# An encoder layer on one core: w_out's parts kept for three passes, a hand-written order of the engines up to the first up tile, and modulation pieces in other places

## The chip, the core and the metric

The kernel runs on one core of a Trainium2 chip. The metric is the device time of one execution in microseconds (us); the median of three executions before the change is 1642.57 us (1640.33 to 1643.46). Four compute engines matter: TensorE (PE) multiplies matrices, VectorE (DVE) and GpSimd (POOL) do elementwise work, ScalarE (ACT) applies functions and copies. SyncE (SP) issues the transfers, in order, on one queue.

## What is computed

One layer with a token mixer and a channel mixer, on 1024 tokens of 1024 features; six modulation rows (shift, scale and gate for each half) come from a small product of a condition vector with w_ada.

```
mod = (silu(c) @ w_ada + b_ada);  sh1, sc1, g1, sh2, sc2, g2 = split(mod, 6)
h = rmsnorm(x) * (1 + sc1) + sh1
z = h @ w_in                                   # q, k, v of three attentions, gates
ya, yb, yc = attention A (chunks), B (forgetting), C (top-k)
merged = sum over b of sigmoid(gate_b) * (y_b @ w_branch[b])
x = x + g1 * rmsnorm(merged @ w_out)
h = rmsnorm(x) * (1 + sc2) + sh2
a, g = split(h @ w_up)                         # 2 x 2816 features
x = x + g2 * rmsnorm((gelu(conv3(a)) * g) @ w_down)
```

## The kernel before

Every large product is made of float32 numbers split in a high and a low part; three matmuls (high x high, high x low, low x high) give one product. Activations stand feature-major (128 features in the partitions, 1024 tokens along), in 8 feature tiles; tokens come in 8 blocks of 128.

Time runs through these stages. Attention (A, B, C with four heads each) runs with a background list, `items`: the projections, 20 early gates (`early_gate`) and modulation pieces (`ada_item`, lines 567 to 576) are worked off a step at a time between the heads' instructions, at a rate per head (`tick`). A modulation piece reads two 128-column strips of w_ada (1 MB, two loads), takes eight VectorE operations over them (`ada_steps`), one GpSimd sum, two small matmuls and two VectorE operations (`ada_end`). There are 16 such pieces for the rows 2 to 5: eight are in `items` (`N_ADA`), the other eight in the merge (lines 1010 to 1016), three per branch.

The merge (lines 972 to 1016) goes over 3 branches x 8 feature tiles: w_branch's parts are split, 12 matmuls per tile make the product, VectorE multiplies it with the gate (line 1000), GpSimd adds it into M (line 1002), and in the last branch M is split and written to DRAM (`M_spill`). Four gates of the last branch (`late_gate`) are made here, 48 matmuls each.

Then w_out (`proj_tokens`, line 1032) in three passes over blocks (0, 1, 2), (3, 4, 5) and (6, 7). A pass loads all eight 128-row strips of w_out again, splits each (ScalarE the high part; GpSimd and VectorE in turn the low part), reads M's strip back (`merged`, in the five places of tag `e`), and makes 6 matmuls per block and strip. `normed` normalises a block's sum from PSUM and adds it to x; `second_norm` normalises again, transposes a block in 8 small matmuls (`xT2`, in the three PSUM banks of tag `n`), applies the modulation and makes the left operands of a seven-product scheme (A11, A12, S1, S2, S4, S3, A22), two blocks (even and odd) for one index i of each left operand. These operands lie in `big` (the two places that held the layer's normalised input) and three `left_S` tiles. The passes' late parts are interleaved in the program with the next pass.

The up projection (`up_tile`, line 1215) goes over 22 feature tiles of a and g: seven products of 12 matmuls each, from `up_weights` (two loads, then right operands B11, B21, T1, T2, B22, T3, T4). The first tile is made in two halves, columns 0 to 255 (blocks 0 to 3) and 256 to 511 (blocks 4 to 7), so that it can start before the last blocks are done. The convolution, GELU and the product follow, and the result goes to DRAM in left operands of the down projection, which is five chunks of seven products (`PLAN`, line 1402), and final blocks. The row of g2 is spread over the partitions (`mod_row(5, ...)`, line 1476) after the first product.

The order of instructions on the engines is made by a planner, from the program's order and modelled times, outside of `manual_schedule`; inside such a section the order of the named engines is the program's own. The planner also allots places (buffers of a tag) and the order of SP's queue in both.

```
    ada_todo = [(a, a + 1) for v in (2, 3, 4, 5) for a in range(v * 8, v * 8 + 8, 2)]
...
    for n_p, blocks in enumerate(((0, 1, 2), (3, 4, 5), (6, 7))):
        o3 = proj_tokens(KD, merged, w_out, blocks, "ddsssn", f"wo{n_p}", 2, (pool, dve))
```

Of the kernel before, what the change touches and what calls it, by code (L numbers as in the profile page):

```python
# [33 lines left out]
N_ADA = 8  # L34
ADA_FROM = 1
# [26 lines left out]
def encoder_layer(ctx: ExitStack, tc: tile.TileContext, x, w_ada, w_in, w_branch, w_out, w_up, w_down,  # L62
# [140 lines left out]
    def ada_end(srcs, acc, tag="n", eng=pool):  # L203

        eng.tensor_tensor(acc[:, 0], acc[:, 0], acc[:, 1], op=OP.add)
        pm = bank(tag, "ada_ps")
# [7 lines left out]
    def ada_piece(srcs, per_k, tag="n"):  # L214
        for acc in ada_steps(per_k):
            pass
        ada_end(srcs, acc, tag)
# [347 lines left out]
    ada_todo = [(a, a + 1) for v in (2, 3, 4, 5) for a in range(v * 8, v * 8 + 8, 2)]  # L565
# [404 lines left out]
    ada_next = None  # L970
    M = [None] * KD
    for b in range(3):
# [5 lines left out]
        for m in range(KD):  # L978
# [31 lines left out]
            if b or m:  # L1010
                if ada_next is not None:
                    ada_piece(*ada_next)
                ada_next = None
# [18 lines left out]
    def proj_tokens(n_k, operand, w, blocks, banks, name, stagger, engs):  # L1032


        tags = iter(banks)
        o = [[bank(next(tags), f"{name}o{t}{e}") for e in range(2)] for t in range(len(blocks))]
        ts_ = slice(blocks[0] * P, (blocks[-1] + 1) * P)
        ops = []
        for k in range(n_k):
            raw = raw4(f"{name}raw{k}", (P, D))  # L1040
            nc.sync.dma_start(raw, w[k * P:(k + 1) * P, :])
            wh, wl = split(raw, (P, D), f"{name}w{k}", engs[k % len(engs)])
            s = operand(k, ts_)
            ops.append((s, wh, wl))
            if k < n_k - stagger:
                steps = [(k, t) for t in range(len(blocks))]
            elif k < n_k - 1:
                continue
            else:
                steps = [(kk, t) for t in range(len(blocks)) for kk in range(n_k - stagger, n_k)]  # L1050
            for kk, t in steps:
                s_, wh_, wl_ = ops[kk]
                tk = slice(t * P, (t + 1) * P)
                for e in range(2):
                    es = slice(e * HALF, (e + 1) * HALF)
                    pe.matmul(o[t][e], s_[:, 0, tk], wh_[:, es], start=(kk == 0), stop=False)
                    pe.matmul(o[t][e], s_[:, 0, tk], wl_[:, es], start=False, stop=False)
                    pe.matmul(o[t][e], s_[:, 1, tk], wh_[:, es], start=False, stop=(kk == n_k - 1))
        return o

    def normed(o, g_row, x1, tmp, name):
# [9 lines left out]
        r = rstd_of(ss, name)  # L1071
        dve.scalar_tensor_tensor(x1, tmp, r, x1, op0=OP.mult, op1=OP.add)
# [19 lines left out]
    h_even = [None]  # L1092

    def second_norm(x1, xn2, tb):
        ss = sm(f"s2_{tb}")
        act.activation(xn2, x1, AF.Square, accum_out=ss)
        r = rstd_of(ss, f"n2_{tb}")
        dve.tensor_scalar(xn2, x1, r, None, op0=OP.mult)
        h32 = (k4 if tb % 2 else f4)(f"h2_{tb}", F32, (P, KD, P))
        for g in range(2):  # L1100
            pt = bank("n", f"xT2_{tb}_{g}")
            for kk in range(4):
                k = g * 4 + kk
# [78 lines left out]
    for n_p, blocks in enumerate(((0, 1, 2), (3, 4, 5), (6, 7))):  # L1182
# [4 lines left out]
        if UP_POS == n_p == 2:  # L1187
            r_first = up_weights(0)
# [339 lines left out]
```

## Time and profile before

| what | value |
|---|---|
| median of 3 executions | 1642.57 us (1640.33 to 1643.46) |
| the profiled execution's own time | 1643.54 us |
| its span, first to last instruction | 1641.7 us |
| TensorE busy | 1513.8 us (92%) |
| VectorE / ScalarE / GpSimd busy | 1207.4 / 805.7 / 594.4 us |
| moved by DMA | 262.37 MB, mean 160 GB/s |
| mean granted clock of TensorE | 0.973 |

The page's picture of the span in 40 equal slices (tenths busy, clock in tenths, 9 for 90% or more):

```
PE   3989999989999999987999849999999999999997
DVE  6766898998678526589536894878777877877768
PEclk9999999999999999998999969999999999999999
```

One slice is 41 us. Read the picture for where TensorE's row falls below 9: at the start, once in attention, in slices 18 and 19 (700 to 780 us, the merge) and 23 and 24 (940 to 990 us, from w_out to the first up tile).

### The profile page before, as it was taken

Reading aid. Unit: us, or ns where it says so; the run is one execution under the profiler, and the core shown is the slowest. Engines: PE = TensorE matmul, PEld = TensorE weight load, DVE = VectorE, ACT = ScalarE, POOL = GpSimd, SP = SyncE. Lnnn points to the kernel's source line nnn. Section 1 sums busy time; section 2 is a strip of 40 time slices with the busy share of each in tenths; the row PEclk is TensorE's granted clock in tenths of the full one; section 3 lists DMA queues with packets and bytes.
Section 4 is the critical chain, followed back from the end, with each engine's and each line's share of the span. In section 5 each row is a group of like instructions: output and inputs, shape, how many; then the busy total and the mean of one; then the engine's idle time right before and its main releaser. Section 6 shows DMA issues by size and latency. Waiting matters only on the chain. (4 is left out here: it accounts for less than half of the span.)

```text
span 1641.7 us, 21382 instructions
## 1 busy us (share of the span) xinstructions
PE 1513.8 (92%) x7322; PEld 1247.1 (76%) x7322; DVE 1207.4 (74%) x2174; ACT 805.7 (49%) x1482; POOL 594.4 (36%) x420
## 2 busy tenths in 40 slices
PE   3989999989999999987999849999999999999997
PEld 2768888777887888765777737778888888788885
DVE  6766898998678526589536894878777877877768
ACT  4434698776544546521235653555555555532212
POOL 3432534443544434116344641222222322432205
PEclk9999999999999999998999969999999999999999
DMA  9442332435452222295668711445444444987752
GB/s 284 123 103 52 97 104 81 155 104 163 122 153 67 77 94 89 86 320 174 211 252 280 241 64 52 141 141 175 146 154 142 141 141 150 407 304 256 260 187 103
DMA packets 190175, 262.37 MB, mean 160 GB/s; under 512 B 15147, under 2 KB 145395, under 8 KB 190067
## 3 DMA queue, kind: packets, MB, share of 16 engines
q1 hardware_dynamic: 190067, 261.01, 48.0%
q8 instruction: 58, 0.95, 0.2%
q14 instruction: 50, 0.41, 0.1%
HBM read 178.14 MB, written 74.97 MB: 154 GB/s over the span
## 5 line engine op out<-in xcount | busy, mean ns | idle before, releaser
L199 DVE SCALAR_TENSOR_TENSOR ada_acc<-ada_raw,c_act,ada_acc 128x256 f32<-128x256 f32 x144 | 99.0, 732 | 4.9 <-DMA ada_raw<-in_w_ada 4.8
L647 ACT ACTIVATE junk<-sc,thr 128x512 bf16<-128x512 f32 (+2 forms) x93 | 80.2, 862 | 30.8 <-DVE thr L668 25.8
L1170 POOL TENSOR_TENSOR T<-ua,ug 128x512 f32<-128x512 f32 x22 | 29.2, 1327 | 175.2 <-DVE rT L1156 166.1
L649 DVE TENSOR_SCALAR_CACHE_REDUCE junk<-sc,thr 128x384 bf16<-128x384 f32 (+2 forms) x93 | 89.6, 964 | 1.8
L1251 POOL TENSOR_TENSOR cv<-cv,g 128x1024 f32<-128x1024 f32 x22 | 58.0, 2639 | 59.2 <-ACT cv L1250 42.5
L1211 PE MATMUL X<-left_S,rT 128*128 128x512 f32 (+1 forms) x184 | 70.8, 385 | 0.5 <-ACT p L1228 0.5
L1213 PE MATMUL X<-left_S,rT 128*128 128x512 f32 (+1 forms) x184 | 70.6, 384 | 0.0
L1212 PE MATMUL X<-left_S,rT 128*128 128x512 f32 (+1 forms) x184 | 70.6, 384 | 0.0
L1471 DVE TENSOR_TENSOR acc<-acc,X 128x512 f32<-128x512 f32 x68 | 46.0, 685 | 24.2 <-PE X L1468 24.2
L1166 POOL TENSOR_TENSOR ug<-ug 128x512 f32<-128x512 f32 x22 | 30.0, 1363 | 86.7 <-DVE ua L1162 86.7
L1341 ACT ACTIVATE T<-work 128x512 fp32r<-128x512 f32 x40 | 25.0, 630 | 59.7 <-PE X L1468 19.6
L1471 DVE TENSOR_TENSOR acc<-acc,V 128x512 f32<-128x512 f32 x56 | 38.1, 685 | 18.0 <-PE V L1468 17.3
L1155 ACT ACTIVATE rT<-ug 128x512 fp32r<-128x512 f32 x44 | 27.5, 625 | 48.3 <-PE X L1213 24.9
L1211 PE MATMUL X<-big,rB 128*128 128x512 f32 (+1 forms) x92 | 36.3, 395 | 15.0 <-DVE xn L1068 14.2
L1467 PE MATMUL X<-T,ring 128*128 128x512 f32 x120 | 47.1, 393 | 0.0
L1466 PE MATMUL X<-T,ring 128*128 128x512 f32 x120 | 46.8, 392 | 0.0
L1468 PE MATMUL X<-T,ring 128*128 128x512 f32 x120 | 46.5, 389 | 0.0
L1156 DVE TENSOR_TENSOR rB<-ua,rB 128x512 fp32r<-128x512 f32 x44 | 37.7, 862 | 9.2 <-ACT rB L1155 8.3
L530 ACT ACTIVATE tg<-g,gate_b 128x512 f32<-128x512 f32 x48 | 32.5, 679 | 22.7 <-PE g L249 22.5
L1156 DVE TENSOR_TENSOR rT<-ug,rT 128x512 fp32r<-128x512 f32 x44 | 33.4, 760 | 12.6 <-ACT rT L1155 12.6
L1341 ACT ACTIVATE B<-wd 128x512 fp32r<-128x512 f32 x26 | 16.4, 631 | 51.8 <-DVE acc L1471 25.9
L1155 ACT ACTIVATE rB<-ua 128x512 fp32r<-128x512 f32 x44 | 27.3, 627 | 29.3 <-PE V L1213 22.3
(1096 smaller groups left out, 5660.0 us busy)
## 6 DMA issues: line engine op xcount, KB each, us to landing
ring<-L_spill SPq DMA_DIRECT2D x70, 512.0 KB, 5.4
L_spill<-S SPq DMA_DIRECT2D x40, 512.0 KB, 4.3
ada_raw<-in_w_ada SPq DMA_DIRECT2D x32, 512.0 KB, 4.5
L_spill<-A SPq DMA_DIRECT2D x30, 512.0 KB, 3.3
raw_g<-in_w_in SPq DMA_DIRECT2D x24, 512.0 KB, 4.1
ua<-in_w_up SPq DMA_DIRECT2D x22, 512.0 KB, 4.0
ug<-in_w_up SPq DMA_DIRECT2D x22, 512.0 KB, 3.8
gate_spill<-tg SPq DMA_DIRECT2D x20, 512.0 KB, 2.6
```

Of the source, the lines that this page charges most:

```text
L199: dve.scalar_tensor_tensor(acc[:, k % 2], per_k[k], c_act[:, k:k + 1], acc[:, k % 2], op0=OP.mult, op1=OP.add)
L647: act.activation(junk_a[:, 0:n], scores[b], AF.Sign, scale=-1.0, bias=t_f, accum_out=cnt[:, j:j + 1])
L649: dve.tensor_scalar(junk_d[:, 0:n], scores[b], t_f, None, op0=OP.is_lt, op1=OP.add, accum_out=cnt[:, j:j + 1])
L1155: act.activation(hl_[0], src, AF.Copy)
L1156: eng.tensor_tensor(hl_[1], src, hl_[0].bitcast(F32), op=OP.subtract)
L1211: pe.matmul(oc, r[:, 0, k], lh, start=(first and k == 0), stop=False, skip_group_check=True)
L1212: pe.matmul(oc, r[:, 0, k], ll, start=False, stop=False, skip_group_check=True)
L1213: pe.matmul(oc, r[:, 1, k], lh, start=False, stop=(last and k == 3), skip_group_check=True)
L1251: pool.tensor_tensor(cv, cv, g, op=OP.mult)
L1466: pe.matmul(o, lh, r[:, 0], start=(starts and k == 0), stop=False, skip_group_check=True)
L1467: pe.matmul(o, lh, r[:, 1], start=False, stop=False, skip_group_check=True)
L1471: dve.tensor_tensor(dst, dst, o, op=OP.add)
```

## The change

w_out's strips are loaded and split once, in pass 0. Strip 0's parts lie in two places of tag `w4`; the parts of strips 1 to 7 lie in places of the left operands for i = 2 and 3, which blocks 4 to 7 fill later. Pass 2 goes over the strips in the order 1, 2, 5, 6, 0, 3, 4, 7. From pass 1 to the last product of the first up tile the order on ScalarE, VectorE, GpSimd and TensorE is written out by hand; SP's is still planned. Even blocks' left operands are made by one ScalarE copy and one VectorE subtraction of double width. The first up tile's right operands lie in other places, `up_weights` gives its steps one by one, and `up_tile` stops after each product. Twelve modulation pieces are in `items` and none in the merge; the four pieces of row 5 are loaded and made in the first three chunks of the down projection, and its row is spread in the fourth.

```
-N_ADA = 8
-ADA_FROM = 1
+ADA_AT = (1, 2, 3, 4, 5, 6, 7, 8, 11, 13, 15, 17)
...
-    ada_todo = [(a, a + 1) for v in (2, 3, 4, 5) for a in range(v * 8, v * 8 + 8, 2)]
+    ada_todo = [(a, a + 1) for v in (2, 3, 4) for a in range(v * 8, v * 8 + 8, 2)]
...
         items.append(early_gate(i))
-        if i >= ADA_FROM and len(ada_todo) > 16 - N_ADA:
+        if i in ADA_AT:
             items.append(ada_item(ada_todo.pop(0)))
...
-            if b or m:
-                if ada_next is not None:
-                    ada_piece(*ada_next)
-                ada_next = None
-                if ada_todo and m in (1, 3, 5):
-                    a = ada_todo.pop(0)
-                    ada_next = (a, ada_load(a, lambda n, shape: f4(n, F32, shape)))
...
+    def wo_load(k, eng):
+        raw = raw4(f"wo_raw{k}", (P, D))
+        nc.sync.dma_start(raw, w_out[k * P:(k + 1) * P, :])
+        if k == 0:
+            hi, lo = (w4(f"wo0{j}", (P, 2, HALF)) for j in "hl")
+        else:
+            hi, lo = (left[n][:, :, i].rearrange("p e k c -> p e (k c)") for n, i in PLACES[2 * k - 2:2 * k])
+        src = raw.rearrange("p (e c) -> p e c", e=2)
+        act.activation(hi, src, AF.Copy)
+        eng.tensor_tensor(lo, src, hi.bitcast(F32), op=OP.subtract)
+        wo.append((hi, lo))
+
+    PLACES = [(n, i) for ns in (("A11", "A12", "A22", "S1"), ("S2", "S4", "S3")) for i in (2, 3) for n in ns]
+
+    class Pass:
+        def __init__(self, n_p, blocks, order):
+            self.n_p, self.blocks, self.order = n_p, blocks, order
+            tags = iter("ddsssn")
+            self.o = [[bank(next(tags), f"wo{n_p}o{t}{e}") for e in range(2)] for t in range(len(blocks))]
+            self.m = {}
+
+        def step(self, n, ts=None):
+            k = self.order[n]
+            if k not in self.m:
+                self.m[k] = merged(k, slice(self.blocks[0] * P, (self.blocks[-1] + 1) * P))
...
+                    pe.matmul(self.o[t][e], s_[:, 0, tk], hi[:, e], start=(n == 0), stop=False)
+                    pe.matmul(self.o[t][e], s_[:, 0, tk], lo[:, e], start=False, stop=False)
+                    pe.matmul(self.o[t][e], s_[:, 1, tk], hi[:, e], start=False, stop=(n == KD - 1))
...
+        def lefts_even(self):
+            h = self.h.rearrange("p (a k) c -> p a k c", a=2)
+            t = big[0]
+            act.activation(t[:, :, 0, self.i], h, AF.Copy)
+            dve.tensor_tensor(t[:, :, 1, self.i], h, t[:, :, 0, self.i].bitcast(F32), op=OP.subtract)
...
-    R0 = dict(B11=e4, B21=e4, T1=e4, T2=w4_first, B22=w4_first, T3=k4_first, T4=raw4)
+    R0 = dict(B11=e4, B21=e4, T1=e4, T2=w4_first, B22=w4_first, T3=w4_first, T4=w4_first)
...
+    pass0 = Pass(0, (0, 1, 2), range(KD))
+    for k in range(KD):
+        wo_load(k, (pool, dve)[k % 2])
+        if k < KD - 2:
+            pass0.step(k)
+    for t in range(3):
+        for k in (KD - 2, KD - 1):
+            pass0.step(k, (t,))
...
+    with tc.manual_schedule(engines={E.Activation, E.DVE, E.Pool, E.PE}):
+        b0, b1, b2 = blocks(0, 1, 2)
+        pass1 = Pass(1, (3, 4, 5), range(KD))
+        b0.normed(pass0.o[0])
+        b0.residual()
+        b1.normed(pass0.o[1])
+        b0.norm2()
+        b1.residual()
+        b0.scaled()
+        b2.normed(pass0.o[2])
+        b1.norm2()
+        pass1.step(0)
+        b0.turn()
+        b1.scaled()
+        b2.residual()
+        b0.modulated()
...
+        r, ws = up_weights(0)
+        go(ws)
+        for n in (4, 5, 6):
+            pass1.step(n)
+        go(ws, 3)
+        b3, b4, b5 = blocks(3, 4, 5)
+        for t in range(3):
+            pass1.step(7, (t,))
+
+        pass2 = Pass(2, (6, 7), (1, 2, 5, 6, 0, 3, 4, 7))
+        b3.normed(pass1.o[0])
+        b3.residual()
+        b4.normed(pass1.o[1])
+        b3.norm2()
+        b4.residual()
+        b3.scaled()
+        b5.normed(pass1.o[2])
+        b4.norm2()
+        pass2.step(0)
+        b4.scaled()
+        b5.residual()
+        b5.norm2()
+        pass2.step(1)
+        b3.turn()
+        b3.modulated()
+        left3 = b3.lefts_odd(b2)
+        go(left3)
+        b5.scaled()
+        pass2.step(2)
+        b4.turn()
+        b4.modulated()
+        go(left3)
+        pass2.step(3)
+        b5.turn()
...
+        pass2.step(6)
+        pass2.step(7, (0,))
+        b6, b7 = blocks(6, 7)
+        b6.normed(pass2.o[0])
+        pass2.step(7, (1,))
+        b6.residual()
+        b7.normed(pass2.o[1])
+        b6.norm2()
+        first = up_tile(0, r, PARTS0)
+        go(first)
+        b7.residual()
+        b6.scaled()
+        go(first)
+        b7.norm2()
+        go(first, 3)
+        b6.turn()
+        b6.modulated()
+        b7.scaled()
+        go(first)
+        b6.lefts_even()
+        b7.turn()
+        b7.modulated()
+        go(first)
...
+    G2_AT = {0: (40,), 1: (42, 44), 2: (46,)}
...
+            if n == 0:
+                for a in G2_AT.get(c, ()):
...
+            if n == 5:
+                for a in G2_AT.get(c, ()):
+                    ada_piece((a, a + 1), ada_in[a], pm=VB[a // 2 % 2])
+                if c == 3:
+                    mod_row(5, G2, VB)
```

`Block` holds the steps that `normed` and `second_norm` made before: `normed` (squares, products with g1's row, the root), `residual` (adds x, writes x1), `norm2` (square and root), `scaled`, `turn` (8 transposes), `modulated`, `lefts_odd` and `lefts_even`; `go` draws the next step of a generator.

## Rows read from the trace of the kernel before

**Rows 1.** Busy time by stretch: stretch, length, five engines (instructions), TensorE's clock, DMA.
```profile
702.00:732.00 30.00, 28.88 (x120) 22.40 (x121) 26.16 (x58) 6.42 (x14) 2.26 (x3) 0.94 0.99 334
732.00:776.00 44.00, 32.43 (x116) 23.34 (x114) 43.71 (x59) 6.66 (x12) 24.73 (x12) 0.88 0.57 183
776.00:841.50 65.50, 63.48 (x275) 52.20 (x276) 30.88 (x39) 18.46 (x24) 28.58 (x13) 0.97 0.61 213
841.50:945.00 103.50, 96.01 (x441) 77.03 (x440) 67.54 (x87) 56.00 (x97) 51.87 (x32) 1.00 0.79 266
945.00:1030.00 85.00, 58.88 (x313) 50.70 (x312) 60.95 (x87) 38.73 (x76) 25.39 (x20) 0.80 0.19 59
960.00:980.00 20.00, 10.53 (x44) 9.32 (x45) 17.54 (x33) 12.48 (x29) 5.07 (x7) 0.51 0.40 131
570.00:630.00 60.00, 60.00 (x321) 50.98 (x321) 19.10 (x60) 27.68 (x54) 20.98 (x16) 1.00 0.23 75
1450.00:1600.00 150.00, 150.00 (x657) 123.09 (x656) 104.62 (x159) 35.47 (x58) 33.11 (x24) 1.00 0.68 240
```

**Rows 2.** TensorE's waits, 700 to 842: us in total, times, longest.
```profile
PE yp L996 <- DVE tgb L1000: 12.9, 8, 2.4
PE ada_ps L208 <- POOL ada_acc L205: 1.4, 1, 1.4
```

**Rows 3.** VectorE by line, 700 to 842: count, busy us, mean ns, idle before.
```profile
L199 DVE SCALAR_TENSOR_TENSOR ada_acc<-ada_raw,c_act,ada_acc 128x256 f32<-128x256 f32 x42 | 33.5, 833 | 0.9 <-DMA ada_raw<-in_w_ada 0.9
L983 DVE TENSOR_TENSOR wb<-wbr,wb 128x256 fp32r<-128x256 f32 x24 | 16.2, 687 | 7.8 <-ACT wb L982 7.8
```

**Rows 4.** TensorE's waits, 838 to 1010.
```profile
PE X L1211 <- DVE xn L1068: 14.2, 1, 14.2
PE xT L1104 <- DVE n L222: 8.5, 3, 4.4
```

**Rows 5.** TensorE by line, 690 to 842.
```profile
L208 PE MATMUL ada_ps<-one,ada_acc 128*128 128x1 f32 x32 | 4.5, 240 | 1.4 <-POOL ada_acc L205 1.4
```

**Rows 6.** VectorE in order of time, 750 to 760: start, duration of the row.
```profile
752.27 3.01 DVE L199 SCALAR_TENSOR_TENSOR ada_acc<-ada_raw,c_act,ada_acc 128x256 f32<-128x256 f32 x2
755.80 0.87 DVE L199 SCALAR_TENSOR_TENSOR ada_acc<-ada_raw,c_act,ada_acc 128x256 f32<-128x256 f32 x2
```

**Rows 7.** TensorE's waits, 300 to 700.
```profile
PE g L247 <- DVE mod L210: 4.0, 2, 2.1
```

**Rows 8.** TensorE in order of time, from 838 and from 930.
```profile
860.43 1.52 PE L1056 MATMUL wo0o<-wo0w4h,m 128*128 128x512 f32 x6
864.51 1.52 PE L1056 MATMUL wo0o<-wo0w5h,m 128*128 128x512 f32 x6
...
932.23 1.09 PE L1104 MATMUL xT<-ident,xn 128*128 128x128 f32 x8 [2.19 <-DVE n L222]
933.08 0.48 PE L1057 MATMUL wo2o<-wo2w4l,m 128*128 128x512 f32 x1
933.39 0.39 PE L1058 MATMUL wo2o<-wo2w4h,m 128*128 128x512 f32 x1
```

**Rows 9.** VectorE by line, 870 to 992.
```profile
L1111 DVE TENSOR_SCALAR h<-xT,mod 128x128 f32<-128x128 f32 x32 | 12.2, 403 | 2.5 <-PE xT L1104 1.6 <-ACT h L1108 0.8
L1122 DVE TENSOR_TENSOR S<-h 128x512 f32<-128x512 f32 x4 | 6.0, 1510 | 0.8 <-ACT h L1108 0.8
L1068 DVE TENSOR_TENSOR xn<-wo0o,G 128x512 f32<-128x512 f32 x6 | 4.0, 688 | 4.6 <-ACT n_0sq L1067 4.5
L1127 DVE TENSOR_TENSOR S<-h,S 128x512 f32<-128x512 f32 x4 | 2.7, 678 | 0.0
L1072 DVE SCALAR_TENSOR_TENSOR x<-xn,n_0r,x 128x1024 f32<-128x1024 f32 x1 | 1.3, 1284 | 0.0
L1098 DVE TENSOR_SCALAR xn<-x,n_6r 128x1024 f32<-128x1024 f32 x1 | 0.8, 756 | 0.7 <-POOL n_6r L224 0.7
```

**Rows 10.** DMA issues: count, KB each, median us to landing.
```profile
m<-M_spill SPq DMA_DIRECT2D x8, 256.0 KB, 4.1
```

More of the change, by code (lines that the diff above doesn't have):

```diff
@@ L1030, in mod_row @@
             act.activation(halves[g], o, AF.Copy)
[L1032 to L1052, printed above, removed]
+    wo = []
@@ new lines, in encoder_layer @@
+    PLACES = [(n, i) for ns in (("A11", "A12", "A22", "S1"), ("S2", "S4", "S3")) for i in (2, 3) for n in ns]
[9 more added lines that the diff above has]
+                self.m[k] = merged(k, slice(self.blocks[0] * P, (self.blocks[-1] + 1) * P))
+            hi, lo = wo[k]
+            s_ = self.m[k]
+            for t in range(len(self.blocks)) if ts is None else ts:
@@ L1053, in proj_tokens @@
                 tk = slice(t * P, (t + 1) * P)
                 for e in range(2):
[L1055 to L1061, printed above, removed]
+                    pe.matmul(self.o[t][e], s_[:, 0, tk], hi[:, e], start=(n == 0), stop=False)
@@ L1070, in normed @@
         dve.tensor_tensor(ss, ss2[:, 0:1], ss2[:, 1:2], op=OP.add)
-        r = rstd_of(ss, name)
-        dve.scalar_tensor_tensor(x1, tmp, r, x1, op0=OP.mult, op1=OP.add)
+        return rstd_of(ss, name)
     G1 = k4("G1")
@@ L1179, in merged @@
         return s
[L1181 to L1204 removed]
+    blk = {}
+    pass0 = Pass(0, (0, 1, 2), range(KD))
+    for k in range(KD):
+        wo_load(k, (pool, dve)[k % 2])
[4 more added lines that the diff above has]
+            pass0.step(k, (t,))
     def product(o, l, r, first, last, c0, c1):
@@ L1218, in up_tile @@
         a, g = e4(f"a{f}"), e4(f"g{f}")
-        for n_part, (c0, c1) in enumerate(parts):
+        for c0, c1 in parts:
             def view(t, odd):
@@ L1303, in down_left, with go, blocks @@
         copied("A22", side(u, 1), to["A22"])
-    r = r_first
-    before = None
-    for f in range(NF):
-        tile_ = up_tile(f, r, PARTS0 if f == 0 else [(0, HALF)])
-        next(tile_)
-        if before is not None:
-            for _ in before:
-                pass
-        if f + 1 < NF:
-            r = up_weights(f + 1)
-        next(tile_)
+    def go(steps, n=1):
+        for _ in range(n):
+            next(steps)
+    def blocks(*tbs):
+        for t in tbs:
+            blk[t] = Block(t)
+        return [blk[t] for t in tbs]
@@ new lines, in encoder_layer @@
+    with tc.manual_schedule(engines={E.Activation, E.DVE, E.Pool, E.PE}):
[14 more added lines that the diff above has]
+        b0.modulated()
+        b2.norm2()
+        pass1.step(1)
+        b1.turn()
+        b0.lefts_even()
+        b2.scaled()
+        b1.modulated()
+        left1 = b1.lefts_odd(b0)
+        pass1.step(2)
+        b2.turn()
+        go(left1, 3)
+        next(left1, None)
+        pass1.step(3)
+        b2.modulated()
+        b2.lefts_even()
+        r, ws = up_weights(0)
[31 more added lines that the diff above has]
+        b5.turn()
+        go(left3)
+        next(left3, None)
+        b4.lefts_even()
+        b5.modulated()
+        pass2.step(4)
+        left5 = b5.lefts_odd(b4)
+        go(left5, 2)
+        pass2.step(5)
+        go(ws, 2)
+        go(left5)
+        next(left5, None)
+        pass2.step(6)
[21 more added lines that the diff above has]
+        go(first)
+        left7 = b7.lefts_odd(b6)
+        go(left7)
+        go(first, 2)
+        go(left7)
+        go(first)
+        go(left7)
+        next(left7, None)
+        r, ws = up_weights(1)
+        go(ws)
+        go(first, 3)
+        for _ in ws:
+            pass
@@ L1316, in encoder_layer @@
+    before = first
+    for f in range(1, NF):
+        tile_ = up_tile(f, r, [(0, HALF)])
+        go(tile_)
+        for _ in before:
+            pass
+        if f + 1 < NF:
+            r, ws = up_weights(f + 1)
+            for _ in ws:
+                pass
+        go(tile_, 5)
         before = tile_
```

180 lines of the change are left out of this document (97 added, 83 removed).

## The prediction

> **What bounds the kernel now.** I read the page's picture of the span first, then the table of stretches [rows 1], then the waits of TensorE in the two stretches where it is not full. The reader is to see in [rows 1] that inside attention (570 to 630) and inside the down projection (1450 to 1600) TensorE is busy for the whole stretch at a clock of 1.00, and that the holes lie between. So the time is TensorE's work plus its holes, and the sum below goes by holes alone.
>
> From 702 to 841.5 (merge of the branches) TensorE is busy 28.88 + 32.43 + 63.48 = 124.8 of 139.5 us [rows 1]: 14.7 idle. [...] With a mean clock c, a share 2(1 - c) of the stretch is at half, and half of the work done there is lost: 28.88 x 0.06 + 32.43 x 0.12 + 63.48 x 0.03 = 7.5. Loss: 22.2 us. Its waits name VectorE's product with the gates, 12.9 [rows 2]; what keeps VectorE there is in [rows 3]: the multiply-adds of the modulation pieces, 33.5 us (42 of their 56 instructions), nearly half of what it has in 732 to 776, where it is full (43.71 of 44).
>
> From 841.5 to 1030 (w_out, second norm, first up tile) TensorE is idle 7.5 + 26.1 = 33.6 us [rows 1], above all 14.2 before the first product of the first up tile and 8.5 before transposes of the normed blocks [rows 4]. Both end with VectorE. In 960 to 980 the clock is 0.51, so almost all of the 10.53 busy there runs at half and half of that, 5.2, is lost; about 1 elsewhere. Loss: 40 us.
>
> **The change part by part.**
>
> *Merge stage: eight modulation pieces leave.* With them go VectorE's 56 instructions of [rows 3], their GpSimd sums, 16 loads of half a megabyte from SP's queue, and TensorE's 32 small matmuls, 4.5 us [rows 5]. What is late next: the first eight tiles (702 to 732) keep about 1.1 idle + 1.7 clock, as that stretch has VectorE free enough and its DMA share of 0.99 falls. The last stretch keeps 2.0 + 1.9. In between, GpSimd adds each product into M. VectorE's operations with two operands in SBUF are held up beside it: two multiply-adds take 3.01 us in one place and 0.87 in the next [rows 6]. The 24 subtractions of w_branch's low parts average 0.69 [rows 3], so they too are held at times. I take 1.5 there: sum 8.2. Bounds: 4 (the first stretch's level, without its clock loss) and 18 (rival 2). Gain 22.2 - 8.2 + 4.5 = 18.5 us, bounds 9 and 23.
>
> *Four pieces go to the gate items in attention.* TensorE's part is 4.5 x 4/8 = 2.25 us, and it is on the path, as TensorE is full there. VectorE has 19.1 of 60 us busy in 570 to 630 [rows 1] and hides its share. Two of the eight pieces already there made TensorE wait for the bank, 4.0 us together [rows 7], so four make 2.0. Cost 4.2; bounds 0 (the pieces fall in a hole) and 8 (each waits 1.5 to 2).
>
> *Four pieces of the last gate row go to the down projection.* Again 2.25 of TensorE, plus 1 for the row's eight transposes, now in a full stretch. VectorE is busy 104.6 of 150 there, so some 45 us are free for four pieces of about 33.5/7 = 5 us. SP issues eight more loads, the first two behind the ring's loads. Cost 3.2. Bounds: 2, and 9 where every piece also holds TensorE for its GpSimd sum (1.4, the one such wait of [rows 2]).
>
> *w_out's parts stay.* 16 of 24 loads (8 MB), their splits on ScalarE, VectorE and GpSimd, and 16 issues of SP go. The places are free only after the last late gate has read its input, just before 841.5; TensorE has step 0 from other buffers meanwhile, 18 matmuls, 4.08 us from one step's first start to the next [rows 8]. If that cover fails, it costs the length of one split, 1 to 2 us. I keep 1 us of idle for pass 0.
>
> *The order by hand.* With 4.08 per step of three blocks, pass 1 is 32.6 us, pass 2 (12 matmuls a step) 21.8, a block's turn 0.85 (932.23 to 933.08) [rows 8]. I followed VectorE's list, since the waits above end there.
>
> Pass 1: with w_out there early, a pass ends block by block, and block 0 is 5.4 us ahead of the pass's end. So its normalisation starts before pass 1 does, and I find 1 us of hole in pass 1.
>
> Pass 2: per block VectorE has two products of 0.69, the residual 1.28, the scaling 0.76 and four of 0.40 [rows 9], 5.0, and about 0.45 of small ones: 16.4 for three blocks. Two odd blocks add six subtractions of 0.68 each, 8.1; the even one and the last w_up parts 1.4 each: 27.3 against TensorE's 21.8 + 3 x 0.85 = 24.4. Six GpSimd operations lie beside it; the same kind of VectorE instruction averages 1.51 at L1122, where GpSimd runs along, and 0.68 at L1127 [rows 9], so +0.85 each: 5 us. Block 4's turn needs a bank that block 3's modulation frees, and on VectorE that stands behind the products and residuals of all three blocks and two scalings: 3 x 2.66 + 2 x 0.76 + 1.6 = 11.1, some 4 for sums and waits for roots (VectorE's share of the 8.5 in [rows 4]), less the 2.7 that block 3 is early: 12.4 against TensorE's three steps and a turn, 9.0. Hole: 4 with rounding up. TensorE then ends pass 2 28 us after pass 1, and VectorE is free for block 6 at about 27.3 + 5 + 3 of waits - 2.7 = 32.6.
>
> Tail: block 6 is thus 4 late; from its products to its turn are 1.4 + 1.3, block 7's 1.4 + 1.3, the scaling 0.8 and some 2 for sums and roots: 8. TensorE has five half-width products of 12 matmuls, 1.36 each, 6.8. Hole: 5. From turn to the second half's products another 8.5 of VectorE and ScalarE against 7.1 of TensorE: 2 with rounding. Behind a held-up VectorE stand the evacuations of the first tile, in its order, so nothing can be drawn ahead there.
>
> *Places.* B11, B21 and T1 of the first tile now take three of the five places that the merged operand is read into, from the middle of pass 1. Two remain: a step must wait for a place to come free and a load of 4.1 us [rows 10]; two steps take 2.72 + 4.1 instead of 5.44, or 0.7 more each, 5.5 for the eight of pass 2. About half lie under holes already counted: 3 us, bounds 0 and 5.5. On SP the first tile's two w_up loads now stand among the merged operand's loads; the DMA share of 0.79 there [rows 1] falls with w_out's 8 MB, so I count nothing for it.
>
> Half clock after these holes: 2, against the 6 of before. Sum: 1 + 1 + 4 + 7 + 3 + 2 = 18; bounds 10 (nothing held, no places) and 35 (rival 1). Gain 40 - 18 = 22, bounds 5 and 30.
>
> On the clock the rows show this: after 2.19 idle and eight transposes TensorE's matmuls lasted 0.39 to 0.48 [rows 8], and the stretch to 945 has a clock of 1.00; after 14.2 idle it ran at 0.51 [rows 1, 4]. [...]
>
> *Sum.* 18.5 + 22 - 4.2 - 3.2 = 33.1. The profiled execution took 1643.54, 1.84 more than its span, which stays: 1610.4. The median is 1.0 lower: **1609 us**. The loop over later tiles only splits at more points and is drawn up to the same ones; TensorE is full there, so I count nothing.
>
> **The rivals.**
>
> 1. *The hand order becomes the bound*: VectorE's list in 841.5 to 1030 stays so late that only 5 us are won. For it: both large waits of before end with VectorE, and in-order lists cannot be reshuffled. Against: sixteen w_out splits are gone, half from VectorE and half from GpSimd, which held VectorE. 1643.5 + 4.2 + 3.2 - 18.5 - 5 - 1 = 1626.
>
> 2. *GpSimd still holds VectorE in the merge.* Every subtraction of w_branch parts that falls beside GpSimd's add waits it out, up to 2.5 (two multiply-adds lost 2.1 together in [rows 6]); for eight tiles 8 x 1.3 more: merge loss 18, gain 9, time 1619. [...] Against the rival: removed pieces were most of what was held.
>
> 3. *Slower: the places.* If one place instead of two remains for the merged operand in pass 2 (a fourth taken early by the first tile's output, which is allotted from the same five), each of 12 steps (four of pass 1, eight of pass 2) lies open with its load, 12 x 4.1 = 49 us, less the 3 counted: 1655. It decides at one place; with two it is the 3 us above. For it: three are held for a third of the stretch. Against: the output is first written after pass 2.
>
> 4. *Better:* VectorE is not held up: 10 us of holes from 841.5 on and 5 in the merge, 1609 - 8 - 3 = 1598.
>
> **How the numbers follow.** Forecast (1600 to 1618) 0.53, rival 1 0.14, rival 2 0.12, rival 3 0.06, rival 4 0.15. The range reaches from inside rival 4 to past rival 1: 1592 to 1630. Anything within 0.2% (3.3 us) of before would be no change by this measurement; it needs rivals 1 and 2 together and worse. Faster 0.91, same 0.02, slower 0.07 (rival 3 and an unnamed rest).
>
> **What would show it.** The table of stretches after: the merge some 18 us shorter, VectorE no longer full in its second third; pass 1 with almost no hole; one hole of 4 us before block 4's transposes and one of about 5 before block 6's, both ended by VectorE; no wait of TensorE for the merged operand over 2 us (rival 3: waits for its DMA at every step of pass 2); clock 1.00 through passes 1 and 2. In attention and in the down projection together 5 to 10 us more. The prediction is wrong if the merge's loss stays over 15, if the holes from 841.5 on exceed 30, or if the later stretches lose more than 12.

## The result and the profile after

The changed kernel takes 1602.17 us (median of 4 executions, 1600.17 to 1603.80) against 1643.01 (4 executions, 1640.33 to 1643.48): ratio 0.9754, 95% interval 0.9737 to 0.9772, about 40 us faster. The forecast was 1609, the range 1592 to 1630. The profiled execution took 1600.86, its span is 1599.1, the mean granted clock 0.984.

From the page of the kernel after: the busy line, and the picture of the span in 40 slices (tenths busy, clock in tenths).

```profile
PE 1497.8 (94%) x7322; PEld 1239.6 (78%) x7322; DVE 1187.5 (74%) x2166; ACT 786.4 (49%) x1462; POOL 561.5 (35%) x408
...
PE   3989999989998999989999999999999999899997
...
DVE  6765888999669854547536779888777777778768
...
PEclk9999999999998999999999999999999999999999
```

The 7 of the merge and the 8 and 4 before the first up tile are gone from TensorE's row. Two 8s are new: slice 35 (from 1359 us), the turn from the up to the down projection, and slice 13 (from 480 us), in attention, where four more pieces are made now.

The table of stretches of the kernel after (start and end, length, busy time with instructions of TensorE, its weight loads, VectorE, ScalarE and GpSimd, granted clock, DMA share, GB/s) answers to [rows 1]: the merge, the three passes and the first tile, the later tiles, the turn.

```profile
702.80:823.80 121.00, 113.88 (x485) 91.31 (x485) 69.27 (x85) 32.91 (x51) 50.10 (x20) 0.99 0.61 208
823.80:860.80 37.00, 36.43 (x163) 29.51 (x161) 14.94 (x19) 12.59 (x24) 11.61 (x7) 1.00 0.86 304
860.80:893.80 33.00, 33.00 (x156) 27.18 (x157) 21.95 (x40) 16.19 (x34) 9.02 (x9) 1.00 0.38 134
893.80:923.60 29.80, 26.36 (x122) 20.17 (x120) 24.95 (x44) 16.88 (x36) 9.23 (x10) 1.00 0.43 150
923.60:955.00 31.40, 27.80 (x192) 26.00 (x193) 22.02 (x39) 15.86 (x37) 8.76 (x9) 0.95 0.21 68
955.00:1010.00 55.00, 54.47 (x246) 44.48 (x246) 47.52 (x57) 30.73 (x50) 17.38 (x10) 1.00 0.40 134
1010.00:1340.00 330.00, 329.51 (x1433) 268.52 (x1432) 261.85 (x332) 176.20 (x282) 92.31 (x52) 1.00 0.44 147
1340.00:1380.00 40.00, 32.54 (x126) 25.79 (x125) 33.24 (x45) 19.92 (x33) 10.56 (x5) 0.87 0.94 351
```

In the merge 7.1 of 121 us are idle, and 113.88 x 0.01 = 1.1 is lost to the clock: a loss of 8.3 where it was 22.2. From the first w_out product to 1010 the idle time is 0.57 + 0 + 3.44 + 3.60 + 0.53 = 8.1, the clock costs 27.80 x 0.05 = 1.4: a loss of 9.5 where it was 40. In the turn, 1340 to 1380, 7.5 us are idle and the clock is 0.87.

TensorE's waits of the kernel after from 823 to 1010 (in all, times, longest), in place of [rows 4]:

```profile
PE X L1246 <- DVE xn L1071: 2.0, 1, 2.0
PE xT L1121 <- ACT h L1128: 1.9, 1, 1.9
PE xT L1121 <- DVE xn L1116: 1.4, 2, 0.8
PE wo2o L1060 <- DMA m<-M_spill: 0.7, 1, 0.7
```

The 14.2 before the first tile's first product has become 2.0, the 8.5 before transposes 1.9 + 1.4.

### The profile page after: what moved, and what is told of

Read it like the earlier page. It is cut to its first block, busy times and chain, and to the rows that moved or that the text cites. A ratio compares the mean times of both kernels' runs of the same rounds, so it can differ in the third digit from the quotient of the medians.

```text
span 1599.1 us, 21251 instructions
## 1 busy us (share of the span) xinstructions
PE 1497.8 (94%) x7322; PEld 1239.6 (78%) x7322; DVE 1187.5 (74%) x2166; ACT 786.4 (49%) x1462; POOL 561.5 (35%) x408
## 4 chain that ended last, share of the span: by engine, by line
PE 63%; DVE 19%; DMA 6%; ACT 5%; issue 4%; POOL 2%; SPq 1%; DVEq 0%; POOLq 0%; ACTq 0%
PE X L1246 4%; PE X L1247 4%; PE X L1248 4%; PE g L247 4%; PE g L248 4%; PE g L249 4%; DVE ada_acc L198 2%; PE X L1627 2%; PE X L1629 2%; PE X L1628 2%; PE V L1246 2%; PE V L1247 2%; PE V L1248 2%; DVE junk L649 2%; PE V L1629 2%
## 5 line engine op out<-in xcount | busy, mean ns | idle before, releaser
L1212 POOL TENSOR_TENSOR T<-ua 128x512 f32<-128x512 f32 x21 | 27.2, 1296 | 174.9 <-DVE rT L1198 165.2
L198 DVE SCALAR_TENSOR_TENSOR ada_acc<-ada_raw,c_act,ada_acc 128x256 f32<-128x256 f32 x120 | 81.4, 725 | 1.3 <-DMA ada_raw<-in_w_ada 1.2
L1501 ACT ACTIVATE T<-work 128x512 fp32r<-128x512 f32 x40 | 25.2, 631 | 63.7 <-PE V L1629 26.9
L1213 POOL TENSOR_TENSOR ug<-ug 128x512 f32<-128x512 f32 x22 | 32.6, 1482 | 66.5 <-DVE ua L1206 66.5
L1001 POOL TENSOR_TENSOR M<-M,tgb 128x1024 f32<-128x1024 f32 x12 | 30.6, 2559 | 68.1 <-DVE tgb L999 68.1
L1197 ACT ACTIVATE rT<-ua 128x512 fp32r<-128x512 f32 x45 | 28.2, 627 | 35.9 <-DVE ua L1210 22.9
L1198 DVE TENSOR_TENSOR rT<-ua,rT 128x512 fp32r<-128x512 f32 x45 | 38.9, 865 | 9.3 <-ACT rT L1197 8.8
L1198 DVE TENSOR_TENSOR rB<-ua,rB 128x512 fp32r<-128x512 f32 x44 | 41.2, 939 | 2.0 <-ACT rB L1197 0.9
L1246 PE MATMUL X<-big,rT 128*128 128x512 f32 (+1 forms) x92 | 36.4, 396 | 5.8 <-DVE g L1278 5.8
L1247 PEld LDWEIGHTS X<-left_S,rT 128*128 128x128 f32 x184 | 34.5, 188 | 7.9 <-DVE left_S L1092 0.4
L615 DVE SCALAR_TENSOR_TENSOR sc<-rl,wi,sc 128x512 f32<-128x512 f32 (+3 forms) x30 | 30.2, 1038 | 14.0 <-ACT rl L614 14.0
```

What stands on the lines that cost most here:

```text
L198: dve.scalar_tensor_tensor(acc[:, k % 2], per_k[k], c_act[:, k:k + 1], acc[:, k % 2], op0=OP.mult, op1=OP.add)
L1198: eng.tensor_tensor(hl_[1], src, hl_[0].bitcast(F32), op=OP.subtract)
L1246: pe.matmul(oc, r[:, 0, k], lh, start=(first and k == 0), stop=False, skip_group_check=True)
L1247: pe.matmul(oc, r[:, 0, k], ll, start=False, stop=False, skip_group_check=True)
```

## The experiments

Every kernel ran in up to six executions beside the kernel before, on one chip per group (e1 to e4, e5 to e8, e9 to e11, e12); ratios are to it, with the 95% interval. Beside the times I cut each profiled execution at the same five instructions, read from the view of a source line or from the timeline: the first merge matmul, the first w_out matmul, ScalarE's first operation on the convolution of the 19th of the 22 up tiles (TensorE is full there, and the turn is still ahead), the last matmul of the final blocks, the end of the span. Stretches in us:

| kernel | ratio, interval | to merge | merge | w_out to tile 19 | tile 19 to last matmul | tail |
|---|---|---|---|---|---|---|
| before | 1 | 702.1 | 139.7 | 520.7 | 266.6 | 12.6 |
| after | 0.9754, 0.9737 to 0.9772 | 702.8 | 120.9 | 487.0 | 276.1 | 12.3 |
| e1 pieces only | 0.9935, 0.9916 to 0.9954 | 706.5 | 121.2 | 521.6 | 275.0 | 12.3 |
| e2 w_out and order only | 0.9782, 0.9761 to 0.9803 | 698.0 | 138.9 | 487.4 | 266.7 | 12.3 |
| e3 last pieces issued later | 0.9739, 0.9720 to 0.9758 | 704.3 | 120.9 | 487.5 | 275.2 | 12.3 |
| e4 all pieces in attention | 0.9694, 0.9676 to 0.9712 | 711.9 | 118.6 | 488.6 | 266.7 | 12.3 |
| e5 planner's order | 0.9739, 0.9717 to 0.9762 | 704.5 | 120.4 | 487.5 | 275.9 | 12.3 |
| e6 last pieces held back | 0.9716, 0.9693 to 0.9739 | 704.0 | 123.1 | 487.4 | 269.9 | 12.3 |
| e7 e4 + load at the turn | 0.9743, 0.9718 to 0.9767 | 712.0 | 117.7 | 487.6 | 269.7 | 12.1 |
| e8 e4 + VectorE work there | 0.9730, 0.9706 to 0.9754 | 710.5 | 117.0 | 489.4 | 266.6 | 12.3 |
| e9 residency only | 0.9949, 0.9933 to 0.9966 | 701.3 | 139.1 | 514.4 | 269.4 | 12.3 |
| e10 e11 + w_out loaded again | 0.9772, 0.9754 to 0.9790 | 704.8 | 120.9 | 494.8 | 269.8 | 12.3 |
| e11 e5 + late first weights | 0.9740, 0.9720 to 0.9760 | 705.7 | 120.9 | 490.0 | 273.3 | 12.3 |
| e12 e5 + old program order | 0.9905, 0.9888 to 0.9922 | 703.6 | 122.0 | 519.4 | 272.9 | 12.2 |

A stretch that an edit doesn't touch shows how far two executions differ: the first, with the same eight pieces, is 702.1, 698.0 and 701.3 (before, e2, e9).

### Two halves: the pieces (e1), and w_out with the order (e2)

e1 is the kernel before with the changed `ada_todo`, `ADA_AT` and `G2_AT`; e2 is the changed kernel with those of before:

```
 e1: before.py            e2: after.py
-N_ADA = 8                -ADA_AT = (1, ..., 17)
+ADA_AT = (1, ..., 17)    +N_ADA = 8
-ada_piece(*ada_next)     +ada_piece(*ada_next)    # merge
+G2_AT = {0: (40,), ...}  -G2_AT = {0: (40,), ...}
```

> The kernel before with the modulation move alone (four pieces more among the gate items, four pieces and the row in the down projection, none in the merge); w_out and the order as before. Theory, that the parts simply add up: the merge gives 18.8, the fill takes 0.7, the pieces' own TensorE work and the row in the down projection take 3, and piece 40 of the last gate row holds VectorE at the turn from up to down and costs 7 there: 8 won, 1635 us. Rival 1, the loss at that turn belongs to the order of the later tiles, not to piece 40: 15 won, 1628. Rival 2, the merge's gain is lost again in w_out because VectorE is the bound there: under 3 won, 1640 or more.

> The changed kernel with the modulation pieces put back where they were: eight in the merge, none in the down projection. What is left of the change is w_out resident and the written order. Theory (parts add up, the loss at the turn from up to down is piece 40's): 30 won from the first w_out product to the second up tile, 1 in the later tiles, 1612 us, and TensorE has no clock below 0.95 at the turn. Rival 1 (that loss belongs to the order): 1619. Rival 2 (the written order lives from VectorE being free after the merge): holes return in the first pass, 1622 or more.

Measured: e1 0.9935 (some 11 us), e2 0.9782 (some 36 us). The table splits the same way whichever half is there already. The merge gains 18.5 (before to e1) and 18.0 (e2 to after). From w_out to tile 19 the other half gains 33.3 (before to e2) and 34.6 (e1 to after). From tile 19 on, the pieces and the row cost 8.4 and 9.4: the loss at the turn comes with the pieces, under either order. Both rivals of e2, and both of e1, fall.

### What the last pieces do at the turn (e3, e4, e6, e7, e8)

```
 e3: after.py
-G2_AT = {0: (40,), 1: (42, 44), 2: (46,)}
+G2_AT = {1: (40, 42), 2: (44, 46)}
```

> The changed kernel with one edit: the four pieces of the last gate row lie two and two in the second and third chunk of the down projection, none in the first. Theory: VectorE is free of piece 40 at the turn from up to down, the wait of 4.8 us for its operation on g and the half clock behind it go, 1595 us (7 less). Rival: the hole is there without the piece (VectorE's list is full at the turn anyway, the DMA queues too) and the time stays at 1602, within 2.

Measured 0.9739: no change, as the rival said. But the trace shows that the edit had not done what it should. VectorE in e3 (start, duration, line, operation):

```profile
1360.04 0.60 DVE L196 TENSOR_SCALAR ada_acc<-work,c_act 128x256 f32<-128x256 f32 x2
...
1363.56 1.49 DVE L198 SCALAR_TENSOR_TENSOR ada_acc<-work,c_act,ada_acc 128x256 f32<-128x256 f32 x1
1364.97 0.68 DVE L1278 TENSOR_TENSOR g<-X,p 128x512 f32<-128x512 f32 x1
1365.57 2.00 DVE L198 SCALAR_TENSOR_TENSOR ada_acc<-work,c_act,ada_acc 128x256 f32<-128x256 f32 x1
```

Piece 40, issued seven products later in the program, still stands at the turn: its place was free, and the planner drew it forward. So e6 gives all four pieces the two places that chunk 0's w_down rows keep until late:

```
 e6: after.py
+G2_AT = {1: (40, 42), 2: (44, 46)}
-spare = iter((work[:, 4 + a % 4], work[:, 5 + a % 4]))
+spare = iter((work[:, 6], work[:, 7]))
```

> The changed kernel with the four last pieces loaded into the two places that the first chunk's w_down rows hold until late in that chunk, so that no VectorE operation of theirs can stand before the last up tile's (in the run with the pieces merely issued later, the planner drew piece 40 back to the turn: its operations stood there at 1360 to 1370). Theory (piece 40's load and VectorE work at the turn cost the 7 us there): no wait of the last tile over 2.5 us, 1595. Rival (the turn loses as much without them): 1602.

(Both pieces of a chunk then work on the second one's columns; the number of operations is the same.) Measured 0.9716, 1595.18; the stretch from tile 19 on takes 269.9 instead of 276.1. The longest wait of the last tile is 1.5. So about 6 of the 9 us go when piece 40 leaves the turn, and some 3 hang on the rest. By time alone the gain is not certain, as the intervals of e6 and after touch (0.9739 and 0.9737).

```
 e4: after.py
-ada_todo = [... for v in (2, 3, 4) ...]
+ada_todo = [... for v in (2, 3, 4, 5) ...]
+ADA_AT = (1, ..., 8, 10, 11, 12, 13, 14, 15, 16, 17)
-G2_AT = ...
```

> The changed kernel with all eight pieces among the gate items of attention, none in the down projection (its row of eight transposes after the first product, as before). Theory: a piece there costs TensorE 0.56 us of its own work and little more, so four more cost 1 to 3; the turn from up to down gives 7 back and the down projection 2: 1595 us. Rival: the pieces now lie so close that each waits for its bank and its VectorE sums, 2 us each, up to 16: 1602 to 1610.

Measured 0.9694, 1595.25 us: faster than the changed kernel, with intervals apart, though the two ran in different groups, and the profiled executions show a span only 1.0 shorter (1598.1 against 1599.1; e4's is the slowest of its five). Four more pieces in attention cost about 7 us (711.9, 712.0 and 710.5 to the merge in e4, e7 and e8, against 704.5 on average over the eight with four fewer), more than the theory's 1 to 3; the 9.4 from tile 19 on come back (276.1 to 266.7).

e7 and e8 add to e4 either the load or the VectorE work of a piece, and nothing else:

```
 e7, after the first product of the down projection
+ada_load((40, 41), ...)               # into work[:, 4], work[:, 5], not read
 e8, at the same place
+for _ in ada_steps([... work[:, 6], work[:, 7] ...]): pass
```

> All eight pieces among the gate items (0.9694 of before, 1593 on before's 1643), plus two loads of half a megabyte that nobody reads, where piece 40's stood at the turn from up to down. Theory (VectorE's work is what costs): within 2 of 1593. Rival (the load costs: the DMA engines are full there, share 1.03, and the ring's loads and w_down stand behind a megabyte, 2.5 us at 400 GB/s): 1596 or more.

> All eight pieces among the gate items (0.9694 of before, 1593 on before's 1643), plus the eight multiply-adds of a piece on VectorE at the turn, on rows of w_down that are there already, without load, sum or matmul; nobody reads the result. Theory (VectorE's work is what costs): the wait of the last tile for its operation on g grows to 4 or more, 1599. Rival (the load): within 2 of 1593.

Measured: e7 0.9743, some 8 us slower than e4, with intervals apart; e8 0.9730, with intervals that touch. Within their own group e7 and e8 aren't apart, and e8 stands 6 us above e4 with no loss in its trace; so what the load costs is read from the traces and not from the 8 us. TensorE's rows with idle time at the turn, first e4, then e7 (start, duration, line; in brackets the idle time before and its end):

```profile
1359.99 0.50 PE L1246 MATMUL V<-left_S,rB 128*128 128x512 f32 x1 [0.62 <-ACT p L1269]
1366.74 0.50 PE L1626 MATMUL X<-B,ring 128*128 128x512 f32 x1 [0.89 <-DMA ring<-L_spill]
1371.04 0.50 PE L1246 MATMUL X<-big,rT 128*128 128x512 f32 x1 [1.52 <-DVE g L1278]
```

```profile
1358.10 0.50 PE L1246 MATMUL V<-left_S,rB 128*128 128x512 f32 x1 [0.60 <-ACT p L1269]
1368.07 0.80 PE L1246 MATMUL X<-big,rT 128*128 128x512 f32 x1 [4.11 <-DVE g L1278]
```

In e4 matmuls of the down projection's first product (`X<-B,ring`) stand before the last tile's last product and cover its wait for VectorE's operation on g. In e7 they are gone from there, the wait is 4.11, and the next matmul takes 0.80 us instead of 0.50. The kernel after shows the same (4.79 at 1365.08, 0.80). So on top of e4 a load alone is enough: with one more megabyte in a stage whose DMA share is 1.02 to 1.03, the planner no longer puts that product ahead, and the stretch grows by 3.0. Where the product does stand ahead, pieces or not, the stretch is 266.6 to 269.9 (before, e2, e4, e6, e8, e9, e10); where it doesn't, 269.7 without piece 40's work on VectorE (e7) and 272.9 to 276.1 with it. VectorE's work alone, with the product ahead, adds nothing in the trace (e8, 266.6); what of e8's ratio is real stays open.

It is the place of that product that decides, and not piece 40 as such: e10 (below) has piece 40's two loads at 1353.7, ahead of the ring's, and its VectorE work from 1365.6 to 1377.1, and the product stands ahead all the same. The stretch is then 269.8, as without piece 40 at the turn (e6, 269.9). From e10:

```profile
1369.42 0.50 PE L1635 MATMUL X<-B,ring 128*128 128x512 f32 x1 [2.60 <-DMA ring<-L_spill]
1372.81 0.50 PE L1256 MATMUL X<-big,rT 128*128 128x512 f32 x1 [1.04 <-DVE g L1288]
```

Why the planner puts the product ahead in one program and not in the other isn't shown.

### What gained the 33 us (e5, e9, e10, e11, e12)

```
 e5: after.py
-with tc.manual_schedule(engines={E.Activation, E.DVE, E.Pool, E.PE}):
+if True:
```

> The changed kernel with the stretch from the second pass to the first up tile given back to the planner (the block that fixes the engines' order is gone, the same instructions are issued in the same program order); w_out stays resident, the modulation pieces stay moved. Theory (the written order is most of the 33 us that the stretch gained, since both large waits of before were VectorE working for other blocks first): the holes before the turns and before the first tile come back, 15 to 25 of the 33 are lost, 1617 to 1627. Rival (w_out's residency is most of it: 16 loads, 16 splits on VectorE and GpSimd gone, no wait for a split): under 8 lost, 1610 or less.

Measured 0.9739: the same as with the written order (0.9754), 487.5 against 487.0 from w_out to tile 19. My theory fell; the planner makes an order as good from the same program. Residency was then the obvious candidate, so I put it into the kernel before alone (e9), and took it out of e5 (e10, with e11 as its control, since the raw rows' three places force the first tile's weights to be prepared late and whole):

```
 e9: before.py, proj_tokens
-    wh, wl = split(raw, (P, D), f"{name}w{k}", engs[k % len(engs)])
+    if k not in wo: wo_load(k, engs[k % len(engs)])      # pass 0 only, into PLACES
 e10: e11 and in Pass.step
+    if self.n_p: wo_again(self.n_p, k, (pool, dve)[k % 2])   # load and split again
 e11: e5
-    go(ws) ... go(ws, 3) ... go(ws, 2)
+    r, ws = up_weights(0); go(ws, 6)                     # before pass2.step(6)
```

> The kernel before with one part of the change: w_out is loaded and split in the first pass alone, into the unfilled left-operand places, and the third pass takes its steps in the changed kernel's order; the planner orders everything as before, the eight pieces stay in the merge. The planner run took the written order off without loss, so two theories are left for the 33 us of this stretch. Theory R (residency: 16 loads, 16 ScalarE copies and 16 subtractions on VectorE and GpSimd gone): 25 to 33 won, 1610 to 1618. Theory S (the finer steps in which the changed kernel issues blocks, lefts and the first tile's weights in program order, and the first tile's operands in other places): under 10 won, 1633 or more.

> The planner's version of the changed kernel with residency undone: in the second and third pass each part of w_out is loaded and split again into its own place, so the 16 loads, copies and subtractions are back; the first tile's weights are prepared in one go late in the third pass, since their raw rows and w_out's share three places. Theory R (residency): 20 or more lost against 1600, 1620. Theory S (steps and places): under 8 lost, 1608 or less.

> The same late and undivided preparation of the first tile's weights, without the reload: what the move alone does, so that the reload's share can be read. Theory R: within 3 of 1600, since the planner can draw the preparation forward. Theory S: 8 or more lost, 1608, because early weights are what lets the first tile start.

Measured: e9 0.9949, 6.3 us less in the stretch; e10 against e11 0.9772 to 0.9740, 4.8 in the stretch. Residency is worth 5 or 6 us there, whichever way it is taken; theory R falls. The late weights alone cost 2.5 (490.0 to 487.5), so the half of theory S about early weights is small. TensorE's largest waits of e9 from 820 to 1030:

```profile
PE xT L1118 <- DVE xn L1112: 13.0, 2, 11.4
PE xT L1118 <- ACT h L1122: 6.1, 3, 3.2
```

With w_out there and the old order, the hole has moved from the first tile's product to a turn, and is as large. That leaves the program's order, or the new splits and places. e12 keeps residency, splits, places and planner, and issues the steps as before: a whole pass, then the whole second norms of the pass before it, then this pass's norms.

```
 e12: e5
+for n_p, tbs in enumerate(((0, 1, 2), (3, 4, 5), (6, 7))):
+    ...                                   # all of p.step, the last two block by block
+    for b in late: b.second_norm()
+    if n_p == 2: r, ws = up_weights(0); go(ws, 6)
+    late = blocks(*tbs)
+    for t, b in enumerate(late): b.normed(p.o[t]); b.residual()
+for b in late: b.second_norm()
```

> The planner's version of the changed kernel (0.9739 of before) with residency, the left operands' new splits and the first tile's new places kept, but issued in the old program order: a whole pass of w_out, then the whole second norms of the pass before, then this pass's norms and residuals; the first tile's weights whole, before the last norms. Theory (the fine program order is what gains, and the planner only follows it): the stretch from w_out to the last up tile returns from 545 to about 570, as with residency alone (570.2), 1624 (1618 to 1630). Rival (the splits and places do it): within 8 of 1600.

Measured 0.9905, 1628.53 us; up to the last up tile, as the expectation has it, it is 573.9, and up to tile 19 the stretch is back at 519.4, close to before's 520.7 and e1's 521.6 although residency, splits and places are there. So the program's order is worth 32 us (519.4 to 487.5) with the rest in place, 29 of them against e11, which prepares the first tile's weights late too (490.0). The new splits and places by themselves gain nothing, and the planner follows the order that it is given. e12 takes the whole fine order back at once; how much of it lies in the passes and how much in the first tile isn't shown. The table of stretches shows how. First e12:

```profile
850.00:880.00 30.00, 30.00 (x132) 24.56 (x131) 10.66 (x21) 7.47 (x18) 3.31 (x6) 1.00 0.56 187
...
910.00:940.00 30.00, 19.84 (x106) 16.60 (x104) 26.88 (x45) 18.50 (x41) 13.65 (x13) 0.84 0.45 149
940.00:970.00 30.00, 25.05 (x156) 23.08 (x157) 26.59 (x41) 15.82 (x32) 9.91 (x8) 0.88 0.17 52
```

and the kernel after, at the same times:

```profile
850.00:880.00 30.00, 29.43 (x142) 24.07 (x141) 22.07 (x43) 17.97 (x39) 7.10 (x9) 1.00 0.53 182
...
910.00:940.00 30.00, 25.88 (x155) 22.83 (x156) 24.34 (x45) 18.58 (x41) 9.73 (x9) 0.94 0.39 132
940.00:970.00 30.00, 29.30 (x169) 25.46 (x169) 22.58 (x30) 14.20 (x26) 10.03 (x7) 1.00 0.13 36
```

VectorE's is the third busy time of a row. In 850 to 880 it has 10.66 us of work in e12 and 22.07 after: the second norms of blocks 0 to 2, issued between the steps of pass 1 and not after the pass. In e12 that work is still to do from 910 on, where VectorE is busy for 26.9 and 26.6 of 30 us and TensorE waits; the single longest wait is 11.9, at 944, in the first tile. The work is the same, it starts earlier.

## Why the prediction was right, step by step

The sum of 33.1 came out some 7 us short of the 40 measured, with two terms off in opposite directions, by some 12 and 6 us: that the forecast lay so near is luck in part.

- **Merge, 18.5 predicted: right in total, not in its parts.** 18.8 in the two profiled executions, 18.0 and 18.5 in the crossed pairs. The loss left, 8.3, is the 8.2 of the sum, but by luck: the first 30 us lose 4.4 to waits and 1.5 to the clock (2.8 in the sum, which took the loads to be in time once the DMA share falls), the middle 2.6 (1.5), the end 0.1 (3.9). Rival 2 (GpSimd holds VectorE) had 18 there and falls. What is late next is a load and ScalarE's copies behind it, not VectorE; the stretches of the kernel after, TensorE's waits in them, and ScalarE's row before the longest:

```profile
702.80:732.80 30.00, 25.65 (x103) 20.25 (x104) 15.90 (x30) 6.08 (x13) 0.00 (x0) 0.94 0.65 215
732.80:768.00 35.20, 32.57 (x137) 25.39 (x138) 30.47 (x31) 8.09 (x14) 26.17 (x11) 1.00 0.55 169
768.00:823.80 55.80, 55.66 (x248) 45.66 (x246) 22.91 (x25) 18.74 (x24) 23.93 (x10) 1.00 0.63 229
```

```profile
PE yp L995 <- ACT wb L981: 4.4, 2, 3.9
PE yp L995 <- DVE tgb L999: 2.6, 3, 1.1
```

```profile
716.60 1.06 ACT L231 ACTIVATE y_0h<-yb 128x1024 fp32r<-128x1024 f32 x1 [8.39 <-DMA yb<-y_spill]
```

- **Four pieces to the gate items, 4.2 predicted: right in size, its wait mis-sized.** The stretch to the merge is 704.5 on average over the eight profiled kernels with twelve pieces, and 700.5 over the three with eight: 4.0. The one pair of before and after shows 0.7; the three with eight pieces differ by 4.1 among themselves. The wait for the bank, 4.0 before [rows 7], was to grow by 2.0 and grew by 5.4 (8.4 to 9.8 in all eight kernels with twelve pieces, 11.4 to 12.4 in the three with sixteen, part of the 7 that their four pieces more cost). That the sum came out is thus luck in part. The kernel after, 300 to 702:

```profile
PE g L247 <- DVE mod L210: 9.4, 4, 5.0
```

- **Down projection, 3.2 predicted: mis-sized, 8.4 and 9.4 measured.** The step that failed is the one on the loads: "SP issues eight more loads, the first two behind the ring's loads", counted at nothing. Piece 40's two stand at 1345 us, ahead of the ring's; e7 shows that such a load alone can move the down projection's first product behind the last tile, and that a wait of 4 is then open. Where the product keeps its place, without piece 40 at the turn (e6, 269.9) or with it (e10, 269.8), 3.2 and 3.1 remain over the 266.7 of e4, which is what the step had. The upper bound of 9 came from another wait, and the result lay at it. With attention's 4.0 the later work lost some 13 by the averages and 10 in the pair, where 5 to 10 was forecast and over 12 was a sign of being wrong.
- **w_out to the first tile, 22 predicted with bounds 5 to 30: mis-sized, 33 to 35 measured up to tile 19**, 30 of it up to 1010 (40 less 9.5). Of the rest, 1.5 is idle time in the later tiles, which the forecast took as full; some 2 aren't placed. The list that I followed for VectorE was right: block 3's modulation should free the bank 12.4 us after pass 1, and the wait ended at 906.4, 12.6 after 893.8; VectorE should be free for block 6 at 32.6, and was at 924.72, at 30.9. The bank itself was freed by ScalarE's half of the modulation, which ran from 904.87, held up behind a square that waited for VectorE's residual of block 5; the forecast named VectorE for it. What failed is the rounding up on top. The hole before block 4's turn was 1.9 and not 4, those in the tail 2.0 + 0.8 + 0.5 + 0.5 and not 7, the places 0.7 and not 3, the passes 0 and 1 0.6 and not 2, the clock 1.4 and not 2. The late start in the tail shows once, before the first product, and so covers the 5 us that I put before block 6's turn as well.
- **VectorE held beside GpSimd, 5 us in pass 2: 3 measured.** The same subtraction of the kernel after beside a GpSimd operation and free, then the GpSimd row beside the first:

```profile
906.55 1.73 DVE L1148 TENSOR_TENSOR S<-h 128x512 f32<-128x512 f32 x1
...
918.49 0.69 DVE L1148 TENSOR_TENSOR S<-h 128x512 f32<-128x512 f32 x1
```

```profile
906.43 1.30 POOL L1149 TENSOR_TENSOR S<-h,h 128x512 f32<-128x512 f32 x1 [0.66 <-ACT h L1128]
```

  It is one of three that were held, by 1.0 each (906.55, 914.91, 923.03); the forecast had six. This extends [rows 6], where the 3.01 us from 752.27 ran beside GpSimd's add into M (752.43 to 755.01), and the 0.87 from 755.80 beside no GpSimd operation.
- **The rivals.** Rival 1 (the hand order as the bound) and rival 3 (places) had no part: the longest wait for the merged operand is 0.7. Rival 4's 10 us of holes and clock is what came in w_out's stretch, though VectorE was held there, and its 5 in the merge did not come; the turn's 6 took the result back to between it and the forecast.
- **What I had wrong about the cause**: I called the gain one of an order by hand, of in-order lists that can't be reshuffled. The planner reaches the same (e5). What counts is the fine order of the program (e12); its trace points to the place of the second norms, which no run takes back alone. Residency is 5 or 6 of the 33 (e9, e10).

The clock's part of a loss, in the sum and above, is busy time x (1 - mean clock), an estimate with two levels, full and half. The trace of the kernel before has them: of the single microseconds from 940 to 990 all read 1.00 or 0.50 but three (0.85, 0.79 and 0.83, where it changes), and the merge's 128x512 matmuls start 0.43 us apart at 0.50 (704 to 706) and 0.23 at 1.00 (708 to 711). By these rows 0.20 of 0.43 is lost, a little less than the half that the sum takes.

The hole of pass 2 cost no clock: the turn behind 1.86 of idle took 0.66 for four transposes, against 0.60 for the four before it, and the granted clock is 1.00 from 893.8 to 923.6.

## What to carry to other kernels

Where a long wait ends with an engine that is full only in that stretch, look for when its work could have started: issuing the norms in fine steps between the matmuls gained some 30 us, with no operation saved, while taking away 16 loads and splits gained 5 or 6. Work moved into a stage with room is to be costed at that stage's edges and for its loads too, and a later place in the program moves nothing if a planner can draw it back: give it a place in memory that comes free late, and read in the trace where it ran.

## What the runs showed of the hardware

In e9 most of the transposes behind a hole ran at a granted clock of 0.50 (956 to 966). TensorE's rows (start, duration, line) before and after its 11.45 us of idle:

```profile
907.34 1.04 PE L1118 MATMUL xT<-ident,xn 128*128 128x128 f32 x8
...
959.96 1.94 PE L1118 MATMUL xT<-ident,xn 128*128 128x128 f32 x8 [11.45 <-DVE xn L1112]
...
967.08 0.42 PE L1226 MATMUL V<-big,rT 128*128 128x256 f32 x1
...
968.98 0.28 PE L1226 MATMUL V<-big,rT 128*128 128x256 f32 x1
```

Eight transposes take 1.94 instead of 1.04 us, those up to 966.72 stay as slow (1.09 and 1.12 for four, behind waits of 1.59 and 1.37), and the matmuls behind them take 0.41 to 0.42 until they fall to 0.28 at 968.98. The granted clock is 0.85 from 966 to 976. The hole's price was thus not over with the first instructions after it. At the turn to the down projection of the kernel after, the first matmul behind 2.67 us of idle took 0.79 and behind 4.79 us 0.80, with a granted clock of 0.76 from 1350 to 1355 and 0.54 from 1365 to 1370; in e4, behind 1.52, it took 0.50, with a clock of 1.00 from 1363 to 1373, and in e10, behind 2.60, 0.50 too, in a slice with 0.9 or more on its page.
